# Gated mixing and dilated attention on one core: early constants, token-major values, ScalarE scales and one Newton chain per pair

## The chip, the cores and the metric

The kernel runs on one core of one Trainium2 chip. The metric is the device time of one launch in microseconds (us). A core has five instruction streams that run side by side and wait for each other by semaphores: PE (matmul, with its weight loads PEld), DVE (VectorE), ACT (ScalarE), POOL (GpSimd) and SP (SyncE, which issues the weight DMAs). Within a stream the instructions start in their written order, and that order is fixed when the program is built.

## The reference, cut to what matters

The program is two blocks of two layers each, on one sequence of 512 tokens and 1024 features in float32: a state-space mixer, a stick-breaking attention, a gated mixer with dilated attention ("even"), a gated linear attention, and a feed-forward part behind each. The change lies in the "even" mixer:

```python
u, v, q, k, vb = split(h @ w_in)                  # five parts of 512 columns each
vn = layer_norm_2(gelu(v))                        # gated mixing, chunks of 128 tokens
mixed = einsum('gts,bnsgc->bntgc', tril(w_s), vn) + b_s
a_out = gelu(u) * mixed
qh, kh, vh = rms_norm(heads(q), q_g), rms_norm(heads(k), k_g), heads(vb)   # 8 heads of 64
for window, dilation in ((128, 1), (512, 4), (2048, 16)):
    o_r, l_r = dilated_branch(qh, kh, vh, window, dilation)   # softmax attention on a strided band
o = sum(softmax over the three l_r) * o_r
return concatenate([a_out, o]) @ w_out
```

The three branches together are one softmax attention in which the weight of a key is multiplied by the number of branches that reach it (0 to 3).

## The kernel before, in words

The stages follow each other: ssm, ffn0, stick, ffn1, even, conv0, gla, conv1. In "even" everything is feature-major: `xh` and `xl` are the high and low parts of the activations, eight tiles of 128 features by 512 tokens, and a projection of 128 output features is 24 matmuls of 128x512 (`mm3`, L239 to L241: high by high, low by high, high by low for eight feature tiles). A projection of all 512 columns in token-major form is `token_proj` (L1190 to L1192): 96 matmuls of the same size, one PSUM bank for each of four blocks of 128 tokens. A weight block arrives by a DMA on SP's queue into `wr`, and is split into `wh` (ACT, L213) and `wl` (DVE, L214).

PSUM has eight banks: two for projections ("mm"), two for accumulations ("acc") and four for the rest ("aux"). Whoever writes into a bank waits until its last reader is done.

`gmlp` computes the gated mixing: `ev_v` by `token_proj`, four blocks of `ev_u`, gelu and layer norm of v (DVE L1234 normalises), the mixing matmuls (L1256 to L1258), ACT L1259, transposes L1263 and DVE L1264. It runs while the tail of ffn1 still finishes its layer norm (L382 to L464).

`dilated` first makes its constants: `dilated_masks` (the count `cnt` and the additive mask `dmask`, L1282 to L1295), the product `gqk` of the two norm gains from a small DMA (`gq`, L1302, L1304), `hsel` and `hrow`, and the zero columns of two value tiles. Then four pairs of heads follow. For each pair:

- `project(n=0)`, k: 24 matmuls; ACT L1322 squares; PE L1325 sums the squares per head (the moments); ACT L1338 copies k times `gqk`; DVE L1344 to L1347 is a chain of 13 small operations with `rstd` in it (three Newton steps), each on the result of the one before; PE L1354 transposes it; ACT L1356 copies (`rt`); PE L1358 broadcasts it; DVE L1359 multiplies; ACT L224 and DVE L225 split into `kh`, `kl`.
- `project(n=1)`, q: 24 matmuls, L1322, L1325, a split into `qh`, `ql` (L1017, L1018) and a Newton chain of its own, which ends in `rq` (L1350).
- `project(n=2)`, v: 24 matmuls and `values` (L1028, four transposes L1031, L1033, L1034).
- `scores` (S0, S1, S2; L1093, L1095): the 10 causal blocks of both heads of the pair, S0 being the largest query block; `weigh` (W, eight pieces of 512, 512, 128, 384, 128, 384, 256, 256 keys): DVE max (L1369), DVE `nb` (L1371), ACT exp (L1372), DVE times `cnt` with a row sum (L1373, called STT below), DVE reciprocal (L1374), DVE division (L1375); `transposed` (T: PE L1054, ACT L1059, DVE L1060); `av` (V: PE L1070 to L1075, ACT L1077, DVE L1078).

The order in which these steps are written is a table, `EVEN_STEPS`, which holds one round of the loop over the pairs; the number after the colon is the distance to the pair of the round. Under it a scheduler puts the instructions of each engine into the final order. "Linear matmuls" below are those of `mm3` and `token_proj`.

Of the kernel before, what the change touches and what calls it, by code (L numbers as in the profile page):

```python
# [8 lines left out]
F32 = mybir.dt.float32  # L9
F32R = mybir.dt.float32r  # L10
# [3 lines left out]
ALU = mybir.AluOpType  # L14
# [17 lines left out]
          + [("ba", 4), ("hg", 2)])  # L32
# [25 lines left out]
    "W01:0 S1:0 W00:0 W10:0 T01:-1 T00:0 T21:-1 V0:-2 P0:1 W11:0 S2:0 P2:0 V1:-1 W20:0 T11:0 T20:0 "  # L58
# [47 lines left out]
class Kern:  # L106
# [279 lines left out]
    def small(self, n=4, dt=F32):  # L386
        return self.nt("small", [P, n], dt, bufs=24)
# [633 lines left out]
    def values(self, ps, vz, scale=None):  # L1021
# [3 lines left out]
        if scale is None:  # L1025
            nc.scalar.activation(vt, ps, AF.Copy)
        else:
            nc.vector.tensor_mul(vt, ps, scale)  # L1028
# [7 lines left out]
    def value_tiles(self, n=2):
        res = []
        for k in range(n):
            t = self.pt(f"vz{k}", [P, 8, 192], F32R)
            self.nc.gpsimd.memset(t.bitcast(F32)[:, :, 0:64], 0.0)  # L1040
            res.append(t)
        return res
# [19 lines left out]
    def av(self, s, vz, wts, e):  # L1062
# [66 lines left out]
    def stick(self):  # L1129
        nc = self.nc  # L1130
        with self.phase("stick") as self.ph:
# [8 lines left out]
            vzs = self.value_tiles()  # L1140
# [54 lines left out]
    def gmlp(self, oh, ol):  # L1195
# [51 lines left out]
        self.linear(bu[len(pu):], self.xh, self.xl, lambda a, pss: evict(a + len(pu), pss))  # L1247

# [24 lines left out]
    def dilated_masks(self):  # L1273

        nc = self.nc
        ps = self.aux()
        for k, n in enumerate((4, 16)):
            a = self.scr()[0:n, :P]
            nc.gpsimd.memset(a, 0.0)
            nc.gpsimd.affine_select(a, a, pattern=[[0, P // n], [-1, n]], compare_op=ALU.not_equal, fill=1.0,  # L1280
                                    base=0, channel_multiplier=1)
            nc.tensor.matmul(ps[:, :P], a, a, start=k == 0, stop=k == 1)  # L1282
        cnt = self.pt("cnt")
        for j in range(4):
# [527 lines left out]
```

## Time and profile before

| | us |
|---|---|
| median of 3 runs (lowest, highest) | 2473.65 (2472.65, 2474.53) |
| the profiled execution | 2473.41 |
| its span in the trace | 2471.7 |
| PE busy over the span | 2405.6 (97%) |
| DVE busy over the span | 1415.8 (57%) |
| ACT busy over the span | 1005.5 (41%) |
| first scores of the four pairs (start of S0) | 1356.81, 1383.87, 1414.43, 1445.32 |
| first matmul of the stage behind "even" (L252) | 1509.18 |

The profiled execution is 1.7 us longer than its span, and 0.24 us under the median. A view by windows gives the busy time of each engine in a stretch; a view of waits gives what the idle time of an engine ended with; a timeline gives single instructions with start, duration, and in brackets the idle time ahead of them with its releaser.

### The profile page before, as it was taken

How to read it: one execution, taken by the hardware profiler on the slowest of the kernel's cores; microseconds unless marked ns; L12 is line 12 of the kernel's file. 1: busy time of each engine (PE TensorE's matmuls, PEld its weight loads, DVE VectorE, ACT ScalarE, POOL GpSimd, SP SyncE). 2: the span in 40 equal slices, each digit the busy share in tenths (PEclk: the TensorE clock that was granted, in tenths of full speed). 3: DMA queues.
4: the chain of work that ended last, by engine and by line, in shares of the span. 5: the costliest groups of instructions: out<-in, count | busy, mean ns of one | idle time of the engine just before them, and what ended most of it. 6: DMA issues, size and time to landing. Idle time of an engine off the chain costs nothing. (4 is left out here: it accounts for less than half of the span.)

```text
span 2471.7 us, 30857 instructions
## 1 busy us (share of the span) xinstructions
PE 2405.6 (97%) x12200; PEld 1993.5 (81%) x12204; DVE 1415.8 (57%) x2544; ACT 1005.5 (41%) x1542; POOL 14.0 (1%) x61
## 2 busy tenths in 40 slices
PE   5999999999999999999999999999999999999999
PEld 4888888888877798888877678888888787888888
DVE  9945633343777874333367886666435677656621
ACT  5843522222655643222244454333325454333321
POOL 0000000000000000000000000000000000000000
PEclk9999999999999999999999999999999999999999
DMA  3522222233211113223322112322332122222332
GB/s 90 110 95 93 79 101 100 95 94 96 77 60 60 43 61 119 97 99 88 102 92 72 48 43 86 111 99 97 94 93 86 55 86 77 94 94 99 93 111 64
DMA packets 99377, 213.50 MB, mean 86 GB/s; under 512 B 44528, under 2 KB 45168, under 8 KB 99232
## 3 DMA queue, kind: packets, MB, share of 16 engines
q1 hardware_dynamic: 99232, 211.53, 27.2%
q8 instruction: 96, 1.57, 0.3%
q14 instruction: 49, 0.40, 0.1%
HBM read 207.04 MB, written 2.10 MB: 85 GB/s over the span
## 5 line engine op out<-in xcount | busy, mean ns | idle before, releaser
L213 ACT ACTIVATE wh<-wr 128x1024 fp32r<-128x1024 f32 (+1 forms) x385 | 400.5, 1041 | 1014.4 <-PE mm L240 405.9
L214 DVE TENSOR_TENSOR wl<-wr,wh 128x1024 fp32r<-128x1024 f32 (+1 forms) x385 | 461.7, 1199 | 448.4 <-ACT wh L213 443.9
L239 PE MATMUL mm<-xh,wh 128*128 128x512 f32 x1016 | 398.9, 393 | 3.5 <-ACT scr L1338 3.1
L241 PE MATMUL mm<-xh,wl 128*128 128x512 f32 x1016 | 398.5, 392 | 0.0
L240 PE MATMUL mm<-xl,wh 128*128 128x512 f32 x1016 | 398.3, 392 | 0.0
L239 PE MATMUL acc<-xh,wh 128*128 128x512 f32 x760 | 296.7, 390 | 0.0
L240 PE MATMUL acc<-xl,wh 128*128 128x512 f32 x760 | 296.3, 390 | 0.0
L241 PE MATMUL acc<-xh,wl 128*128 128x512 f32 x760 | 296.0, 389 | 0.0
L239 PEld LDWEIGHTS mm<-xh,wh 128*128 128x128 f32 x1016 | 191.4, 188 | 44.9 <-ACT scr L1338 3.5
L240 PEld LDWEIGHTS mm<-xl,wh 128*128 128x128 f32 x1016 | 191.3, 188 | 39.5 <-issue 0.2
L241 PEld LDWEIGHTS mm<-xh,wl 128*128 128x128 f32 x1016 | 191.4, 188 | 39.0 <-issue 0.6
L240 PEld LDWEIGHTS acc<-xl,wh 128*128 128x128 f32 x760 | 143.0, 188 | 29.7 <-issue 0.2
L241 PEld LDWEIGHTS acc<-xh,wl 128*128 128x128 f32 x760 | 143.0, 188 | 29.5
L239 PEld LDWEIGHTS acc<-xh,wh 128*128 128x128 f32 x760 | 143.0, 188 | 29.4
L239 PE MATMUL mm<-hh,wh 128*128 128x512 f32 (+1 forms) x396 | 145.0, 366 | 1.0 <-DVE v L353 1.0
L239 PE MATMUL acc<-hh,wh 128*128 128x512 f32 (+1 forms) x396 | 145.1, 366 | 0.5 <-DVE v L353 0.5
L240 PE MATMUL acc<-hl,wh 128*128 128x512 f32 (+1 forms) x396 | 145.0, 366 | 0.0
L240 PE MATMUL mm<-hl,wh 128*128 128x512 f32 (+1 forms) x396 | 145.0, 366 | 0.0
L241 PE MATMUL acc<-hh,wl 128*128 128x512 f32 (+1 forms) x396 | 144.7, 365 | 0.0
L241 PE MATMUL mm<-hh,wl 128*128 128x512 f32 (+1 forms) x396 | 144.7, 365 | 0.0
L239 PEld LDWEIGHTS mm<-hh,wh 128*128 128x128 f32 x396 | 74.6, 189 | 13.6 <-DVE v L353 1.4
L239 PEld LDWEIGHTS acc<-hh,wh 128*128 128x128 f32 x396 | 74.6, 189 | 13.1 <-DVE v L353 0.9
(489 smaller groups left out, 3891.0 us busy)
## 6 DMA issues: line engine op xcount, KB each, us to landing
wr<-down_dram SPq DMA_DIRECT2D x64, 448.0 KB, 3.3
wr<-gu_g_dram SPq DMA_DIRECT2D x44, 512.0 KB, 3.2
wr<-gu_u_dram SPq DMA_DIRECT2D x44, 512.0 KB, 3.2
wr<-gate_dram SPq DMA_DIRECT2D x44, 512.0 KB, 3.2
wr<-up_dram SPq DMA_DIRECT2D x44, 512.0 KB, 3.2
wr<-down_dram SPq DMA_DIRECT2D x32, 512.0 KB, 3.6
wr<-sb_qkv_dram SPq DMA_DIRECT2D x24, 512.0 KB, 3.2
wr<-glu_dram SPq DMA_DIRECT2D x16, 512.0 KB, 3.3
```

The lines of the kernel that those rows point to most:

```text
L213: nc.scalar.activation(hi[:, :cols], raw[:, :cols], AF.Copy)
L214: nc.vector.tensor_sub(lo[:, :cols], raw[:, :cols], hi[:, :cols])
L239: nc.tensor.matmul(ps[:, c0:c1], wh[:, s], xh[k][:, c0:c1], start=st, stop=False)
L240: nc.tensor.matmul(ps[:, c0:c1], wh[:, s], xl[k][:, c0:c1], start=False, stop=False)
L241: nc.tensor.matmul(ps[:, c0:c1], wl[:, s], xh[k][:, c0:c1], start=False, stop=en)
```

## The change

- `even_consts` takes the place of `dilated_masks`: counts, mask, `hsel`, `hrow` and `gqk` are written ahead of `gmlp`, in tiles of their own; the gains come with the table of parameter columns that is loaded at the start of the program, so the DMA `gq` is gone.
- The values are projected token-major for all pairs at once, by `token_proj` of `ev_vb` in `gmlp` behind `ev_u` and ahead of the mixing (`even_values`), and are written straight into one tile `vz`. `project(n=2)`, its four transposes per pair and the step P2 are gone.
- In `gmlp` the normalisation of v goes from DVE to ACT (L1230), with one DVE operation more for its bias.
- In `weigh` the piece's `nb` and its final division go from DVE to ACT (L1374 and L1378 of the kernel after).
- The moments of k and q share a bank, and one Newton chain of 16 columns, behind q's moments, serves both; `rq` and `nrq` come by ACT (L1352, L1353).

```diff
 EVEN_STEPS = (
-    "W01:0 S1:0 W00:0 W10:0 T01:-1 T00:0 T21:-1 V0:-2 P0:1 W11:0 S2:0 P2:0 V1:-1 W20:0 T11:0 T20:0 "
+    "W01:0 S1:0 W00:0 W10:0 T01:-1 T00:0 T21:-1 V0:-2 P0:1 W11:0 S2:0 V1:-1 W20:0 T11:0 T20:0 "
     "W21:0 T10:0 P1:1 S0:1"
...
+        nb = self.small(4)
+        V.scalar_tensor_tensor(nb, ag[:, 0:8:2], -1.0, r, op0=ALU.mult, op1=ALU.mult)
         for n, v in enumerate(vg):
-            V.tensor_scalar(v, v, ag[:, 2 * n:2 * n + 1], r[:, n:n + 1], op0=ALU.subtract, op1=ALU.mult)
+            nc.scalar.activation(v, v, AF.Identity, scale=r[:, n:n + 1], bias=nb[:, n:n + 1])
...
         self.linear(bu[len(pu):], self.xh, self.xl, lambda a, pss: evict(a + len(pu), pss))
+        self.even_values()
...
+    def even_values(self):
+
+        nc = self.nc
+        pss = self.token_proj([("ev_vb", u) for u in range(4)], self.xh, self.xl)
+        for tb, ps in enumerate(pss):
+            r = self.rcol[:, tb:tb + 1]
+            src = ps.rearrange("p (n d) -> p n d", d=64)
+            h, l = (self.vz[:, tb, :, k:k + 64] for k in (64, 128))
+            nc.scalar.activation(h, src, AF.Copy, scale=r)
+            nc.vector.scalar_tensor_tensor(l, src, r, h, op0=ALU.mult, op1=ALU.subtract)
...
-            st = self.aux()
-            moments(ps, st, 0)
-            if n == 0:
-                kr = self.scr()
-                nc.scalar.activation(kr, ps, AF.Copy, scale=gqk)
-            else:
-                s["q"] = self.split_psum(ps, "q", 2)
-            var = self.small(8)
...
+            if n == 0:
+                s["st"] = self.aux()
+            moments(ps, s["st"], 8 * n)
+            if n == 0:
+                s["kr"] = self.scr()
+                nc.scalar.activation(s["kr"], ps, AF.Copy, scale=gqk)
                 return
+            s["q"] = self.split_psum(ps, "q", 2)
+            s["v"] = self.vz[:, :, 2 * hp:2 * hp + 2]
+            var = self.small(16)
...
-                V.scalar_tensor_tensor(nb, mx, -1.0, sc, op0=ALU.mult, op1=ALU.mult)
+                nc.scalar.activation(nb, mx, AF.Copy, scale=st["nrq"][:, 2 * qb + e:2 * qb + e + 1])
                 nc.scalar.activation(pq, zq, AF.Exp, scale=sc, bias=nb)
                 V.scalar_tensor_tensor(pq, pq, 1.0, cnt[:, T - kv:], op0=ALU.mult, op1=ALU.mult, accum_out=den)
                 V.reciprocal(den, den)
-                V.tensor_scalar(pq, pq, den, None, op0=ALU.mult)
+                nc.scalar.activation(pq, pq, AF.Copy, scale=den)
...
     def even(self):
-        with self.phase("evout") as self.op:
+        with self.phase("evout") as self.op, self.phase("evc") as self.ph2:
+            self.ph = self.ph2
             oh, ol = [None] * NM, [None] * NM
+            self.even_consts()
+            self.vz = self.pt("vz", [P, 4, 8, 192], F32R)
+            self.nc.gpsimd.memset(self.vz.bitcast(F32)[:, :, :, 0:64], 0.0)
```

The final order of the engines moves in three places that matter here. First ACT in the middle of the first pair, where the pieces of `weigh` follow each other; `aux` are score banks, `scr` the weights, L213 is a weight split and L1059 (L1051 after) a transposed copy. Before:

```order
L1372 ACTIVATE scr_11344<-aux_11214,small_11346,small_11151 128x128
L224 ACTIVATE kh_11340<-scr_11307 128x512
L1372 ACTIVATE scr_11344<-aux_11214,small_11355,small_11151 128x384
L1372 ACTIVATE scr_11373<-aux_11363,small_11375,small_11151 128x256
L1059 ACTIVATE wth_11383<-aux_11385 128x128
```

After, the same pieces:

```order
L1375 ACTIVATE scr_11386<-aux_11291,small_11388,small_11252 128x128
L1374 ACTIVATE small_11397<-small_11396,small_11253 128x1
L1378 ACTIVATE scr_11386<-scr_11386,small_11389 128x128
L1375 ACTIVATE scr_11386<-aux_11291,small_11397,small_11252 128x384
L1374 ACTIVATE small_11417<-small_11416,small_11253 128x1
L1378 ACTIVATE scr_11386<-scr_11386,small_11398 128x384
L1375 ACTIVATE scr_11415<-aux_11405,small_11417,small_11252 128x256
```

Between two exps (L1372 before, L1375 after) now stand the next piece's `nb` (L1374) and the division of the piece before (L1378), and the split of the next pair's k (L224) is no longer among them.

Second, DVE behind the last piece of the first pair: its STT (L1373 before, L1376 after), then the work for the next pair up to the first max (L1369, L1372). `ql` is the low part of q, `wtl` a transposed copy. Before:

```order
L1373 SCALAR_TENSOR_TENSOR scr_11399,small_11402<-scr_11399,cnt_10982 128x256
...
L1018 TENSOR_TENSOR ql_11457<-mm_11424,qh_11456 128x512
L1060 TENSOR_TENSOR wtl_11261<-aux_11409,wth_11260 128x3x128
L1344 TENSOR_TENSOR small_11460<-aux_11449,rsq_11003 128x8
...
L1347 TENSOR_TENSOR small_11478<-small_11478,cst_63 128x8
L1350 TENSOR_SCALAR small_11481<-small_11478 128x8
L1369 TENSOR_REDUCE small_11494<-aux_11484 128x1
```

After:

```order
L1376 SCALAR_TENSOR_TENSOR scr_11441,small_11444<-scr_11441,cnt_10484 128x256
L1347 TENSOR_TENSOR wide_11501<-aux_11377,small_11148 128x16
L1377 RECIPROCAL small_11444<-small_11444 128x1
L1348 TENSOR_SCALAR wide_11501<-wide_11501 128x16
L1020 TENSOR_TENSOR ql_11498<-mm_11466,qh_11497 128x512
...
L1350 TENSOR_TENSOR wide_11519<-wide_11519,cst_63 128x16
L1362 TENSOR_TENSOR scr_11384<-scr_11384,aux_11533 128x512
L225 TENSOR_TENSOR kl_11537<-scr_11384,kh_11536 128x512
L1372 TENSOR_REDUCE small_11551<-aux_11541 128x1
```

Before, only q's chain stood there, and k's chain, the product L1359 and the split L225 stood in the middle of the pieces; now the common chain, the product (L1362) and the split (L225) all stand between the last STT of one pair and the first max of the next.

Third, PE at the same place: transposes of the weights (L1054 before, L1046 after), the moments of the next q (L1325, L1330), and S0 of the next pair (L1095, L1087). Before:

```order
L1054 MATMUL aux_11394<-ident_58,scr_11373 128x128 x2
L1054 MATMUL aux_11409<-ident_58,scr_11241 128x128 x4
L241 MATMUL mm_11577<-xh_10215,wl_11574 128x512
L1325 MATMUL aux_11449<-hsel_10998,scr_11450 128x2 x4
L1095 MATMUL aux_11483<-kh_11340,qh_11456 128x512
```

After, with 12, 4 and 7 linear matmuls in the places left out:

```order
L1046 MATMUL aux_11436<-ident_58,scr_11415 128x128 x2
L1046 MATMUL aux_11451<-ident_58,scr_11318 128x128 x4
L1330 MATMUL aux_11377<-hsel_10513,scr_11491 128x2 x4
...
L1356 MATMUL aux_11526<-ident_58,wide_11519 2x128 x4
...
L1360 MATMUL aux_11533<-scr_11531,hrow_10514 128x512
...
L1087 MATMUL aux_11540<-kh_11536,qh_11497 128x512
```

The transposes of the chain (L1356) and the broadcast (L1360) of the next pair's k have moved from the middle of the pieces to the stretch between the last q moments and S0.

## Rows read from the trace of the kernel before

**Rows 1.** The page, busy time of the engines and share of the span.

```profile
PE 2405.6 (97%) x12200; PEld 1993.5 (81%) x12204; DVE 1415.8 (57%) x2544; ACT 1005.5 (41%) x1542; POOL 14.0 (1%) x61
```

**Rows 2.** Windows: length, busy PE, PEld, DVE, ACT, POOL, granted PE clock, DMA.

```profile
1285.00:1300.00 15.00, 12.94 (x55) 9.81 (x56) 14.46 (x35) 14.90 (x35) 0.00 (x0) 1.00 0.22 71
...
1339.00:1346.00 7.00, 3.57 (x20) 2.73 (x19) 5.03 (x17) 4.49 (x11) 2.62 (x8) 0.74 0.23 74
```

**Rows 3.** Windows cut at the four S0 and at the next stage's first matmul.

```profile
1356.81:1383.87 27.06, 25.61 (x136) 18.61 (x136) 20.85 (x79) 13.76 (x25) 0.00 (x0) 1.00 0.19 59
1383.87:1414.43 30.56, 29.43 (x162) 21.36 (x162) 25.77 (x94) 15.08 (x28) 0.00 (x0) 1.00 0.16 52
1414.43:1445.32 30.89, 29.95 (x164) 21.99 (x165) 26.66 (x95) 16.43 (x29) 0.00 (x0) 1.00 0.16 51
1445.32:1509.18 63.86, 61.39 (x295) 47.78 (x296) 46.96 (x111) 30.41 (x49) 0.00 (x0) 1.00 0.19 67
```

**Rows 4.** Waits of PE from 1290 to 1720: total, times, longest.

```profile
PE mm L239 <- ACT scr L1338: 3.1, 1, 3.1
PE aux L1054 <- DVE scr L1375: 2.3, 2, 1.3
...
PE aux L411 <- DVE acc L464: 1.1, 1, 1.1
```

**Rows 5.** Timeline of PE behind the longest wait: start, duration, instruction.

```profile
1345.64 0.63 PE L240 MATMUL mm<-xl,wh 128*128 128x512 f32 x1
...
1349.06 0.43 PE L239 MATMUL mm<-xh,wh 128*128 128x512 f32 x1
```

**Rows 6.** Timeline of PE in a run of linear matmuls, 21 starts apart.

```profile
1312.09 0.39 PE L241 MATMUL acc<-xh,wl 128*128 128x512 f32 x1
...
1316.86 0.39 PE L241 MATMUL acc<-xh,wl 128*128 128x512 f32 x1
```

**Rows 7.** Timeline of DVE, first pair: STT of pieces 1, 4, 5, 8.

```profile
1361.97 0.69 DVE L1373 SCALAR_TENSOR_TENSOR scr<-scr,cnt 128x512 f32<-128x512 f32 x1 [2.19 <-ACT scr L1372]
...
1368.29 0.55 DVE L1373 SCALAR_TENSOR_TENSOR scr<-scr,cnt 128x384 f32<-128x384 f32 x1
...
1375.24 0.28 DVE L1373 SCALAR_TENSOR_TENSOR scr<-scr,cnt 128x128 f32<-128x128 f32 x1
...
1381.98 0.41 DVE L1373 SCALAR_TENSOR_TENSOR scr<-scr,cnt 128x256 f32<-128x256 f32 x1
```

**Rows 8.** Timeline of DVE, Newton chain of the second pair's q, 12 starts apart.

```profile
1385.99 0.16 DVE L1345 TENSOR_SCALAR small<-small 128x8 f32<-128x8 f32 x1
...
1388.39 0.17 DVE L1350 TENSOR_SCALAR small<-small 128x8 f32<-128x8 f32 x1
```

**Rows 9.** Groups of DVE by line and shape, 1340 to 1460: busy, mean ns.

```profile
L1369 DVE TENSOR_REDUCE small<-aux 128x1 f32<-128x512 f32 x8 | 5.5, 684 | 0.0
L1371 DVE SCALAR_TENSOR_TENSOR small<-small,small 128x1 f32<-128x1 f32 x29 | 4.5, 155 | 0.1
```

**Rows 10.** Groups of ACT by line and shape, 1340 to 1460.

```profile
L1372 ACT ACTIVATE scr<-aux,small,small 128x512 f32<-128x512 f32 x8 | 6.2, 777 | 16.5 <-DVE small L1371 16.5
...
L1372 ACT ACTIVATE scr<-aux,small,small 128x128 f32<-128x128 f32 x8 | 3.6, 455 | 13.6 <-DVE small L1371 13.6
...
L1338 ACT ACTIVATE scr<-mm,gqk 128x512 f32<-128x512 f32 x4 | 2.8, 692 | 2.1 <-DVE small L1345 2.1
L224 ACT ACTIVATE kh<-scr 128x512 fp32r<-128x512 f32 x4 | 2.5, 632 | 4.8 <-DVE scr L1359 4.8
...
L1356 ACT ACTIVATE rt<-aux 2x512 f32<-2x512 f32 x4 | 2.3, 584 | 4.0 <-PE aux L1354 4.0
...
L1372 ACT ACT_TABLE_LOAD x1 | 1.3, 1283 | 2.3 <-DVE small L1371 2.3
L1285 ACT ACTIVATE cnt<-aux 128x128 f32<-128x128 f32 x4 | 0.9, 278 | 0.4 <-PE aux L1282 0.4
```

**Rows 11.** Timeline of DVE in ffn1's tail: the low split of the mixing weights.

```profile
1279.12 1.23 DVE L225 TENSOR_TENSOR wsl<-wsr,wsh 128x1024 fp32r<-128x1024 f32 x1
```

More of the change, by code (lines that the diff above doesn't have):

```diff
@@ L1019, in split_psum, with values @@
         return hi, lo
-    def values(self, ps, vz, scale=None):
+    def values(self, ps, vz):
         nc = self.nc
         vt = self.scr()
-        if scale is None:
-            nc.scalar.activation(vt, ps, AF.Copy)
-        else:
-            nc.vector.tensor_mul(vt, ps, scale)
+        nc.scalar.activation(vt, ps, AF.Copy)
         tr = self.aux()
@@ L1032, in values @@
         src = tr.rearrange("p (b d) -> p b d", d=64)
+        vz = vz.rearrange("p t e d -> p (t e) d")
         nc.scalar.activation(vz[:, :, 64:128], src, AF.Copy)
         nc.vector.tensor_sub(vz[:, :, 128:192], src, vz[:, :, 64:128])
[L1036 to L1042, printed above, removed]
     def new_wt(self):
@@ L1271, in out_pair, with even_consts @@
         return h, l
-    def dilated_masks(self):
+    def even_consts(self):
         nc = self.nc
[L1276 to L1284, printed above, removed]
-            nc.scalar.activation(cnt[:, j * P:(j + 1) * P], ps[:, :P], AF.Copy, bias=1.0 if j == 3 else 0.0)
-        own = cnt[:, 3 * P:]
-        nc.gpsimd.affine_select(own, own, pattern=[[-1, P]], compare_op=ALU.is_ge, fill=0.0, base=0,
-                                channel_multiplier=1)
-        near = self.scr()[:, :P]
-        nc.gpsimd.memset(near, 1.0)
-        nc.gpsimd.affine_select(near, near, pattern=[[1, P]], compare_op=ALU.is_ge, fill=0.0, base=0,
-                                channel_multiplier=-1)
-        nc.vector.tensor_add(cnt[:, 2 * P:3 * P], cnt[:, 2 * P:3 * P], near)
-        mask = self.pt("dmask", [P, T], BF16)
-        nc.vector.tensor_scalar(mask, cnt, 0.5, -1e30, op0=ALU.is_lt, op1=ALU.mult)
-        return cnt, mask
@@ new lines, in even_consts @@
+        cnt, mask = self.pt("cnt"), self.pt("dmask", [P, T], BF16)
+        with self.phase("evt") as ph:
+            ps = self.aux()
+            near = ph.tile([P, P], F32, name=self.nm("near"), tag="near", bufs=1)
+            nc.gpsimd.memset(near, 1.0)
+            nc.gpsimd.affine_select(near, near, pattern=[[1, P]], compare_op=ALU.is_ge, fill=0.0, base=0,
+                                    channel_multiplier=-1)
+            for k, n in enumerate((4, 16)):
+                a = ph.tile([P, P], F32, name=self.nm("sel"), tag="sel", bufs=2)[0:n]
+                nc.gpsimd.memset(a, 0.0)
+                nc.gpsimd.affine_select(a, a, pattern=[[0, P // n], [-1, n]], compare_op=ALU.not_equal, fill=1.0,
+                                        base=0, channel_multiplier=1)
+                nc.tensor.matmul(ps[:, :P], a, a, start=k == 0, stop=k == 1)
+            for j in range(4):
+                nc.scalar.activation(cnt[:, j * P:(j + 1) * P], ps[:, :P], AF.Copy, bias=1.0 if j == 3 else 0.0)
+            own = cnt[:, 3 * P:]
+            nc.gpsimd.affine_select(own, own, pattern=[[-1, P]], compare_op=ALU.is_ge, fill=0.0, base=0,
+                                    channel_multiplier=1)
+            nc.vector.tensor_add(cnt[:, 2 * P:3 * P], cnt[:, 2 * P:3 * P], near)
@@ new lines, in even_consts @@
+        nc.vector.tensor_scalar(mask, cnt, 0.5, -1e30, op0=ALU.is_lt, op1=ALU.mult)
+        hsel, hrow, gqk = self.pt("hsel", [P, 2]), self.pt("hrow", [2, P]), self.pt("gqk", [P, 1])
+        nc.gpsimd.memset(hsel, 0.0)
+        for e in (0, 1):
+            nc.gpsimd.memset(hsel[64 * e:64 * e + 64, e:e + 1], 1.0 / 64)
+        nc.gpsimd.memset(hrow, 0.0)
+        nc.gpsimd.affine_select(hrow, hrow, pattern=[[-1, 2], [0, 64]], compare_op=ALU.not_equal, fill=1.0,
+                                base=0, channel_multiplier=1)
```

64 lines of the change are left out of this document (27 added, 37 removed).

## The prediction

> **What bounds the kernel now.** The page first: PE is busy 97% of the span, DVE 57%, ACT 41% [rows 1]. So a change can gain at most what PE still waits, and it can lose wherever it makes PE wait. Next the windows of the stage: in the four attention pairs PE is busy 25.6 of 27.1, 29.4 of 30.6 and 29.9 of 30.9 us, and 61.4 of 63.9 in the last stretch [rows 3]. Then the list of waits: the one long wait is 3.1 us for the copy of k (ACT L1338), which needs `gqk` and so the DMA of the gains [rows 4]. Behind it the granted clock is low: 0.74 over 1339 to 1346 [rows 2], and eight matmul starts take 3.42 us, 0.43 each [rows 5], the lower of the two levels (1.2 GHz), against (1316.86 - 1312.09)/21 = 0.227 in a run at the upper one, 2.4 GHz [rows 6]. Some nine matmuls at 0.2 too much are 1.8 us.
>
> The point that decides comes last: PE is nearly full in the pairs because the projections of the coming pair, 72 matmuls of 0.227 = 16.3 us, fill it while DVE and ACT work off the softmax. That softmax is a chain of its own. In the first pair it runs from S0 at 1356.81 to the STT of piece 1 at 1361.97 (5.2 us), to that of piece 8 at 1381.98 (20.0 us) and to the next S0 at 1383.87 (1.9 us) [rows 3, 7]. PE and this chain take about the same time; whoever shortens one alone gains nothing, and whoever lengthens one pays.
>
> **Early constants and gains.** The wait of 3.1 us and the 1.8 us of low clock behind it have no cause any more: `gqk` is there long before. Gain 4.9. The mixing no longer waits for v's normalisation, since 96 matmuls lie ahead of it: 0.3 at most, taken.
>
> The same edits put work into ffn1's tail. By the order, the splits of the mixing weights (1.23 us on DVE [rows 11], about as much on ACT) move from ahead of the layer norm's last chain to 1285 to 1300, where DVE is busy 14.46 and ACT 14.90 of 15 us [rows 2]; L411, which there ends a 1.1 us wait for DVE L464 [rows 4], comes that much later. `cnt` and `dmask` stand inside the chain ahead of it, each at most a 512-wide operation (0.69). The chain itself starts earlier by the split that left. Together I take 1.6, between -0.5 (all of it hidden, the chain early) and +2.5 (all of it on the path). The memset of `vz` and the selects on POOL wait for nobody that PE needs before the first S0; if that cover were gone they would cost a few us once.
>
> **Values in one go.** `token_proj` puts 96 matmuls, 21.8 us, ahead of the first S0. By the order the first S0 moreover has 31 more matmuls of k1 and q1 ahead of it and 24 (v of pair 0) fewer: 103 in all, 103 x 0.227 = 23.4 us. Four transposes fewer are 0.4. The chain from q's moments to S0 of the first pair is covered by only about 20 matmuls now: 0.8. So the first S0 moves by 23.4 - 4.9 - 0.3 - 0.4 + 1.6 + 0.8 = **+20.2 us**. This is no loss as long as the pairs get shorter by the same amount: 3 x 24 value matmuls leave them (16.3 us), and 31 of the next pair's go ahead (7.0). DVE L1028 and L1034 go too.
>
> **The pieces of `weigh`.** From one STT to the next the order now demands STT, max of the next piece, its `nb` on ACT, the division of this piece on ACT, the next exp. For two 512-wide pieces: STT 0.69 [rows 7], max 0.68 [rows 9], `nb`, division 0.69 (as L1338, which also reads a column as scale), exp 0.78 [rows 10]: 2.84 without `nb`. `nb` on ACT is not in the trace; it lies between DVE's 0.16 [rows 9] and ACT's 128 x 128 copy with a further 0.1 for the column operand, 0.38 (L1338 against 0.59 to 0.6 for plain 512-wide copies such as L1356 [rows 10]); one column being far from 128, I take 0.22. So 3.06. For the other widths I take the lines between the 512 and the 128 rows (STT and max 0.55, 0.41, 0.28; exp 0.67, 0.56, 0.46; division 0.59, 0.48, 0.38): 2.33, 2.10, 2.10, 2.10, 2.33, 2.08. Seven steps: **16.1 us**. With `nb` and division left on DVE, the latter off the chain, the same sum is 12.9. In the trace the seven took 20.0, of which 6.95 went between pieces 4 and 5 [rows 7], where the order had k's Newton chain on DVE and its copy `rt` on ACT ahead of the exp. That work leaves the pieces. The other six took 1.8 more than their sum (a weight split in between); I take 0.7 of it again, from 0 to 1.8: 16.8.
>
> A rule of the Trainium skill bears on `nb`. The page "ScalarE: Activation LUTs" ("What ACT_TABLE_LOAD costs") gives an activation 186 ns, plus 93 ns for a column operand; that estimate is 0.28, and by it 28 pieces would be 1.7 us longer than by mine.
>
> **One Newton chain per pair.** In the order it stands behind the last STT, since q's moments (PE) do, and everything up to S0 hangs on it: q's moments behind the last transposes 1.0; 13 operations of 0.20 [rows 8] with `ql` and two `wtl` pieces among them, 4.0; four small transposes 0.7; `rt` 0.58 [rows 10]; the broadcast, one fp32 matmul of 512, as four passes of 0.227: 1.0 (this and the transposes are estimates from rows 6); the product 0.68; `kh` 0.63 [rows 10]; five hand-overs of 0.1. Sum **9.1 us** where the trace has 1.9. From 7 (nothing else between) to 11 (a weight split of 1.2 and a wait for it). What saved 13 operations on DVE saves none on this path: k's chain lay inside the pieces, beside their waits.
>
> **The pairs.** S0 to the first STT stays 5.2 in the first pair and is 3.9 in the others, which have no table load (1.28 [rows 10]). Pair 1: 5.2 + 16.8 + 9.1 = 31.1. Pair 2: 3.9 + 16.8 + 9.1, and 1.8 for a weight split and the copies of the pair before on the path: 31.6. Pair 3, with 1.0 of these: 30.8. Together 93.5 against 88.5 [rows 3]: **+5.0**, although PE has 23 us less to do there. PE waits some 10 us per pair.
>
> **The last stretch.** 3.9 + 16.8 to the last STT, 5.7 for its division, transposes, copies, values and output split, then by the order about 154 linear matmuls (35.0): 61.4 against 63.9, **-2.4**.
>
> **Sum.** 20.2 + 5.0 - 2.4 = 22.8; on the profiled execution's 2473.4 (0.24 under the median, which changes nothing) this is **2496 us**, slower by 0.9%. The bounds, `nb` on both ends included, give 2486 to 2506.
>
> **Rivals.** *PE keeps the bound* (faster). If the chain fits beside PE's work, the pairs cost what PE does in them: 85.0 busy [rows 3] - 16.3 - 7.0 = 61.6 instead of 88.5, and the time is 2473.4 + 20.2 + 61.6 - 88.5 = 2467. It decides from 22.8 us per pair downward ((88.5 - 20.2)/3). For it: DVE is busy only 20.9 to 26.7 us per pair [rows 3] and loses about 7 of that. Against it: 16.1 for the pieces and 7 for the k chain are already more, and they stand in a row. This is also what a rule of the skill would make of it: "Perfetto Trace Analysis" ("Optimizing Scalar/DVE Operations") recommends handing work to Scalar if DVE is saturated. Here DVE has idle time, and the pieces wait on single results. The same section speaks for breaking instructions up where engines that are not saturated make bubbles elsewhere, which is the reverse of one 16-wide chain; by that rule the forecast stands. Chance 0.10.
>
> *The k chain hides* (no change). If moments and chain slip between the pieces, 3 us remain of the 9.1, the pairs take about 75, and 20.2 + 75 - 88.5 - 2.4 = +4.3 with the bounds of the pieces gives 2470 to 2478. For it: q's matmuls are done early. Against it: the order on DVE. Chance 0.09.
>
> *The clock falls in every pair* (slower still). PE's waits are then longer than the 3.1 us that went with a low clock here; at 1.8 each for three pairs 2501, with more falls up to 2508. For it: rows 5. Against it: matmuls stand between the waits. Chance 0.20.
>
> *The change is not what it says*: the order shows each part at its place. Chance 0.01.
>
> **How the numbers follow.** Forecast 0.60, the rivals 0.10, 0.09, 0.20, 0.01. Predicted is the forecast's 2496. The range leaves out the PE bound and the lower half of the hidden chain below and little above: 2477 to 2508. A measurement can tell about 0.2% from no change, 2469 to 2478. Faster: 0.10; same: 0.08, nearly all of the hidden chain; slower: 0.82.
>
> **What would show it.** Right: the wait for the k copy and the low clock at 1342 gone; first S0 near 1377; S0 to S0 near 31 us with PE busy about 21 of it; DVE idle between the STTs ending on ACT; DVE's 16-wide chain behind the last STT and PE idle there for several us. Wrong: S0 to S0 under 25 us, or the STTs of a pair under 14 us from first to last, or the common chain finished before the last STT. A first S0 after 1380 would blame the constants in ffn1's tail; a granted clock under 0.9 in the pairs speaks for the third rival.

## The result and the profile after

The changed kernel takes 2515.3 us (median of 4 runs, 2510.8 to 2525.5) against 2473.8: 1.0176 times the time of before, 95% interval 1.0152 to 1.0200. I had forecast slower, 2496 in a range of 2477 to 2508. The direction held; the loss is 41 us where I had 22, and lies outside the range. Executions of one kernel lie up to 15 us apart and a trace shows only one of them: for after, e7, e13 and e15 one that is 4 to 5 us under the kernel's median, for e1, e2, e3, e5 and e10 one that is 3 to 7 us over it.

The profiled execution took 2510.82 us, 37.4 more than that of before. Its windows, cut as [rows 3] are, show where (columns as there: length, busy PE, PEld, DVE, ACT, POOL, granted PE clock, DMA):

```profile
1375.99:1413.26 37.27, 30.34 (x128) 21.42 (x129) 16.71 (x57) 19.13 (x41) 0.00 (x0) 0.82 0.10 32
1413.26:1447.90 34.64, 27.67 (x139) 19.84 (x139) 18.53 (x60) 20.09 (x44) 0.00 (x0) 0.95 0.09 31
1447.90:1483.56 35.66, 27.20 (x120) 18.77 (x122) 17.95 (x61) 18.51 (x43) 0.00 (x0) 0.81 0.04 16
1483.56:1549.36 65.80, 56.63 (x252) 44.33 (x254) 39.80 (x78) 33.92 (x63) 0.00 (x0) 0.87 0.17 56
```

The first S0 starts 19.2 us later than before (1375.99 against 1356.81). The three pairs take 107.6 us instead of 88.5, the last stretch 65.8 instead of 63.9. That is 40.2 at the first matmul of the next stage; 2.8 come back behind it. DVE's busy time per pair fell from between 21 and 27 us to between 17 and 19, as intended, and the granted clock fell from 1.00 to 0.82, 0.95, 0.81 and 0.87. PE is busy 85.2 us in the three pairs, as before (85.0), though the records show 387 matmuls there instead of 462: a part of them ran at the lower clock.

The list of PE's waits follows, in the same stretch as [rows 4] (total, times, longest). The copy of k is gone from it, and in its place stands the division of the weights on ACT (L1378), for which the transposes (L1046) wait:

```profile
PE aux L1046 <- ACT scr L1378: 21.1, 8, 4.4
PE aux L1087 <- ACT kh L224: 2.9, 2, 1.4
PE mm L239 <- DVE ql L1020: 2.8, 3, 1.1
...
PE aux L413 <- DVE acc L466: 2.2, 1, 2.2
```

The next lines are from the timeline of DVE in the first pair: the STT (L1376) of pieces 1, 2, 7 and 8, the first operation of the common Newton chain, and the product for the next k (they answer to [rows 7]):

```profile
1380.93 0.69 DVE L1376 SCALAR_TENSOR_TENSOR scr<-scr,cnt 128x512 f32<-128x512 f32 x1 [2.51 <-ACT scr L1375]
...
1383.87 0.69 DVE L1376 SCALAR_TENSOR_TENSOR scr<-scr,cnt 128x512 f32<-128x512 f32 x1 [1.57 <-ACT scr L1375]
...
1394.32 0.43 DVE L1376 SCALAR_TENSOR_TENSOR scr<-scr,cnt 128x256 f32<-128x256 f32 x1 [1.25 <-ACT scr L1375]
...
1401.09 0.41 DVE L1376 SCALAR_TENSOR_TENSOR scr<-scr,cnt 128x256 f32<-128x256 f32 x1
...
1403.59 0.17 DVE L1347 TENSOR_TENSOR wide<-aux,small 128x16 f32<-128x16 f32 x1 [2.08 <-PE aux L1330]
...
1411.53 0.69 DVE L1362 TENSOR_TENSOR scr<-scr,aux 128x512 f32<-128x512 f32 x1 [4.25 <-PE aux L1360]
```

Six of the seven steps of this pair take 13.4 us together; I had 14.0. The seventh takes 6.8, where I had 2.1. (In the second pair the fourth step takes 4.8, in the third the fifth 5.7 and the seventh 4.0.) ACT's timeline shows what it waits for: the division of piece 7 (L1378) stands behind a copy of transposed weights (L1051) and a weight split (L213), and the copy waits 3.5 us for PE:

```profile
1397.82 0.28 ACT L1051 ACTIVATE wth<-aux 128x128 fp32r<-128x128 f32 x1 [3.53 <-PE aux L1046]
1398.06 1.06 ACT L213 ACTIVATE wh<-wr 128x1024 fp32r<-128x1024 f32 x1
1399.02 0.49 ACT L1378 ACTIVATE scr<-scr,small 128x256 f32<-128x256 f32 x1
```

And PE's timeline shows why it is late there. It stood 3.3 us for the division of piece 2, then ran moments, scores and linear matmuls at the low clock (two starts 0.43 apart), and the transposes that ACT waits for stand behind those matmuls:

```profile
1385.78 0.66 PE L1046 MATMUL aux<-ident,scr 128*128 128x128 f32 x4 [3.29 <-ACT scr L1378]
...
1390.85 0.63 PE L240 MATMUL mm<-xl,wh 128*128 128x512 f32 x1
1391.28 0.63 PE L241 MATMUL mm<-xh,wl 128*128 128x512 f32 x1
...
1397.30 0.49 PE L1046 MATMUL aux<-ident,scr 128*128 128x128 f32 x3
```

Two windows give the clock: the place of [rows 2] is at the full clock now, and inside the first pair it is 1.2 GHz for most of 8 us.

```profile
1339.00:1346.00 7.00, 7.00 (x33) 5.79 (x32) 2.45 (x2) 2.92 (x3) 0.00 (x0) 1.00 0.30 85
1386.00:1394.00 8.00, 7.83 (x29) 5.68 (x28) 4.23 (x18) 5.93 (x16) 0.00 (x0) 0.58 0.20 66
```

So ACT waits for PE, which waited for ACT, and each round is made longer by the clock that the wait brings. The 2.8 us that come back later go with a low stretch that the trace of before has near 1935 (0.72 over 1930 to 1942) and this one has not.

### The profile page after: what moved, and what is told of

Its sections match the earlier page's. It is cut to its first block, busy times and chain, and to the rows that moved or that the text cites. A ratio compares the mean times of both kernels' runs of the same rounds, so it can differ in the third digit from the quotient of the medians.

```text
span 2509.1 us, 30756 instructions
## 1 busy us (share of the span) xinstructions
PE 2419.3 (96%) x12184; PEld 2004.0 (80%) x12188; DVE 1393.8 (56%) x2417; ACT 1030.6 (41%) x1618; POOL 14.6 (1%) x60
## 5 line engine op out<-in xcount | busy, mean ns | idle before, releaser
L213 ACT ACTIVATE wh<-wr 128x1024 fp32r<-128x1024 f32 (+1 forms) x385 | 400.4, 1041 | 1024.4 <-PE mm L240 413.4
L214 DVE TENSOR_TENSOR wl<-wr,wh 128x1024 fp32r<-128x1024 f32 (+1 forms) x385 | 461.7, 1200 | 460.2 <-ACT wh L213 456.1
L239 PE MATMUL mm<-xh,wh 128*128 128x512 f32 x984 | 387.5, 394 | 2.3 <-DVE ql L1020 1.9
L240 PE MATMUL mm<-xl,wh 128*128 128x512 f32 x984 | 386.1, 392 | 0.0
L241 PE MATMUL mm<-xh,wl 128*128 128x512 f32 x984 | 385.5, 392 | 0.0
L239 PEld LDWEIGHTS mm<-xh,wh 128*128 128x128 f32 x984 | 185.9, 189 | 43.0 <-DVE ql L1020 2.1
L241 PEld LDWEIGHTS mm<-xh,wl 128*128 128x128 f32 x984 | 185.6, 189 | 39.4 <-issue 1.9
L240 PEld LDWEIGHTS mm<-xl,wh 128*128 128x128 f32 x984 | 185.8, 189 | 39.0 <-issue 0.8
L239 PEld LDWEIGHTS mm<-hh,wh 128*128 128x128 f32 x396 | 74.7, 189 | 13.5 <-DVE v L353 1.4
L239 PEld LDWEIGHTS acc<-hh,wh 128*128 128x128 f32 x396 | 74.6, 188 | 13.1 <-DVE v L353 0.9
```

What stands on the lines that cost most here:

```text
L213: nc.scalar.activation(hi[:, :cols], raw[:, :cols], AF.Copy)
L214: nc.vector.tensor_sub(lo[:, :cols], raw[:, :cols], hi[:, :cols])
L239: nc.tensor.matmul(ps[:, c0:c1], wh[:, s], xh[k][:, c0:c1], start=st, stop=False)
L240: nc.tensor.matmul(ps[:, c0:c1], wh[:, s], xl[k][:, c0:c1], start=False, stop=False)
L241: nc.tensor.matmul(ps[:, c0:c1], wl[:, s], xh[k][:, c0:c1], start=False, stop=en)
```

## The experiments

Each kernel's ratio is to runs of the kernel before on the same chip (medians 2472.9 to 2474.0). "After" with a part undone, or "before" with one thing added.

### One part at a time

**e1**: the kernel before with the constants early.

```diff
+            self.even_consts()
...
-        cnt, mask = self.dilated_masks()
-        gq = self.load("gq", [P, 2], i["ev_qkg"], eng=nc.sync, pool=self.ph)
+        cnt, mask, hsel, hrow, gqk = self.evc
```

> The kernel before, with its constants and the product of the gains made early and nothing else changed (values, scales, Newton chains, normalisation as before). If the early constants do what the prediction says, the wait of 3.1 us for the k copy and the low clock behind it (1.8) go and ffn1's tail costs 1.6: 2473.8 - 3.3 = 2470.5, faster by 0.13%. Rival: the work in ffn1's tail eats the whole gain, 2473 to 2476, with the wait at L413 1.5 us longer or more.

2475.4 us, 1.0018 (1.0008 to 1.0028). The gain that I had booked isn't there. The wait for the k copy is gone. The trace has new low stretches in the first two pairs (0.87 and 0.85), and they take 32.0 and 33.9 us instead of 27.1 and 30.6; but the trace took 2481.8 us, 6.4 over the median, so what takes the gain at the median is not shown.

**e2**: after, with `nb` and division on DVE again.

```diff
-                nc.scalar.activation(nb, mx, AF.Copy, scale=st["nrq"][:, 2 * qb + e:2 * qb + e + 1])
+                V.scalar_tensor_tensor(nb, mx, -1.0, sc, op0=ALU.mult, op1=ALU.mult)
...
-                nc.scalar.activation(pq, pq, AF.Copy, scale=den)
+                V.tensor_scalar(pq, pq, den, None, op0=ALU.mult)
```

> The kernel after with nb and the division of weigh back on DVE; values early and the common Newton chain stay. If the two ACT operations per piece lengthen the chain of the pieces and block ACT's queue, the seven steps fall from 20.2 (1380.93 to 1401.09 in the first pair) to 14 to 15 us and the time to 2515 - 4 x 5 = 2495. Rival (the common chain and the lost value matmuls are what costs, and the pieces only move the idle time): 2508 to 2515.

2517.7 us, 1.0191 (1.0172 to 1.0209). My first reading of the trace after, that ACT's two operations per piece make the loss, falls: without them the seven steps take 20.1 to 25.0 us in the four pairs, and the time is the same.

**e3**: after, with a Newton chain each for k and q. **e4**: after, with the values per pair.

```diff
-            var = self.small(16)
+            var = self.small(8)
...
-            r = self.rstd(var, 16)
+            r = self.rstd(var, 8)
```

> The kernel after with a Newton chain each for k and q as before; scales on ACT and values early stay. If the common chain is what stands between the last piece and the next S0, that stretch falls from 12.2 us (1401.09 to 1413.26) to 3 or 4, and k's chain goes into the pieces: 3 x 8 saved, some 3 x 3 given back there, about 2500. Rival (PE at the low clock and ACT's queue set the stretch): within 4 us of 2515.

2498.2 us, 1.0109 (1.0094 to 1.0125): 17 us back, as expected. From the last STT to the next S0 it is 3.5, 3.4 and 3.5 us, and the seven steps take 22.1, 26.0 and 23.4, together 9.9 more than in after. The edit also gives k's and q's moments a bank each again, so it doesn't part the chain from the shared bank.

```diff
-        self.even_values()
...
+            if n == 2:
+                s["v"] = vzs[hp % 2]
+                self.values(ps, s["v"], self.rrow)
+                return
```

> The kernel after with the values projected per pair as before, inside the attention; scales on ACT and the common chain stay. If PE merely lacks work in the pairs, the 72 value matmuls fill its idle time again: first S0 near 1358, pairs still 31 to 36 us, clock near 1.0, time 2515 - 23 - 6 (clock) = 2486. Rival (the chain and its queues grow with the values' four transposes and copies on ACT and DVE): pairs of 38 us and more, 2495 to 2505.

2495.2 us, 1.0093 (1.0078 to 1.0108): 20 us back, but by the rival's way. The first S0 goes back to 1353.1, the clock doesn't recover (0.95, 0.72 and 0.92), and the pairs take 35.9, 41.7 and 40.5.

### Do the parts add up?

**e5** undoes e3's and e4's parts together, **e6** keeps only the values (and early constants), **e7** only the common chain. The edits are those above.

> Undoes two parts at once: values per pair and a Newton chain each for k and q, as before; scales on ACT, early constants and the normalisation on ACT stay. If the costs of the early values (2515 - 2495 = 20) and of the common chain (2515 - 2498 = 17) add up, 2515 - 37 = 2478. If they are one cost with two names (either alone makes the pairs a chain with PE idle), undoing both brings little more than undoing one: 2488 to 2494.

2473.6 us, 1.0009 (1.0000 to 1.0019).

> Early constants, early values and the normalisation on ACT alone: the scales of weigh are on DVE and k and q have a Newton chain each, as before. The price of the early values by themselves. If they only pay for PE work that the pairs can't get back (21.8 us into the front, chain of 30 us per pair unchanged): 2475 + 20 = 2495. Rival: without ACT's two operations per piece the pairs shorten to 25 us, since PE has 16 us less to do in them: 2480.

2496.8 us, 1.0102 (1.0087 to 1.0118).

> Early constants, the common Newton chain and the normalisation on ACT; values per pair and scales on DVE as before. The price of the common chain by itself. If it stands on the path behind the last piece: 2475 + 3 x 5 to 6 = 2492. Rival (it costs only where ACT's scales block the queue too): 2475 to 2480.

2492.7 us, 1.0088 (1.0071 to 1.0104).

With after and e1 to e4 that is every combination of three parts (all have the early constants, and all but e1 the normalisation on ACT):

| scales on ACT | values early | common chain | us |
|---|---|---|---|
| no | no | no | 2475.4 (e1) |
| yes | no | no | 2473.6 (e5) |
| no | yes | no | 2496.8 (e6) |
| no | no | yes | 2492.7 (e7) |
| yes | yes | no | 2498.2 (e3) |
| yes | no | yes | 2495.2 (e4) |
| no | yes | yes | 2517.7 (e2) |
| yes | yes | yes | 2515.3 (after) |

The values cost 20 to 25 us in every pair of rows that differ in them alone, the chain 17 to 22, the scales between -2.4 and +2.5, and the costs add up within 3 us. In e6 the pairs take 31.0, 34.5 and 33.6 us, in e1, with 72 more matmuls in them, 32.0, 33.9 and 31.8: PE's work leaves the pairs and the pairs don't notice. (The granted clock of these pairs is 0.88, 0.80 and 0.75 in e6, and 0.87, 0.85 and 1.00 in e1, so a lower clock may be a part of the reason; the table doesn't part the two.) In e7 the eight STTs take 17.9, 18.0 and 27.0 us from first to last (e1: 24.2, 26.1 and 24.7), but from the last STT to the next S0 it is 11.8, 13.5 and 9.5 (e1: 3.6, 2.2 and 2.2).

### More and less work for PE

**e8**: after, with a fourth product in the projections of k and q. **e9**: after, without their third product (the weights' low part doesn't enter k and q). **e13**: the fourth product twice. **e12**: the fourth product in the kernel before.

```diff
-            ps, = self.group([(bk, bq)[n][hp]], self.xh, self.xl)
+            w = (bk, bq)[n][hp]()
+            ps = self.mm()
+            (wh, wl), k0, nk = w[0]
+            self.mm3(ps, w, self.xh, self.xl, last=False)
+            for j in range(nk):
+                c = slice(j * P, (j + 1) * P)
+                nc.tensor.matmul(ps, wl[:, c], self.xl[k0 + j], start=False, stop=j == nk - 1)
```

> The kernel after with a fourth product in the projections of k and q (low weights by low activations, 8 more matmuls each): 64 more matmuls, 14.5 us of PE work, 28 of them (6.4 us) ahead of the first S0 and the rest in the pairs. If the pairs are a chain of ACT and DVE with idle PE, only the 6.4 us show, less whatever the fuller PE wins at the clock: 2515 to 2522. If PE or its place in the queues sets the pairs, all shows: 2530 or more.

2508.8 us, 1.0160 (1.0138 to 1.0183): with 14.5 us more work for PE no slower. The median is 6 us lower, but the intervals overlap. The first S0 starts where that of after does (1375.97), so nearly all of the 64 matmuls stand in the pairs (442 matmuls recorded there, 387 in after), and not 28 of them ahead as I had expected. Windows from S0 to S0:

```profile
1375.97:1410.09 34.12, 32.10 (x158) 22.48 (x159) 17.93 (x58) 18.87 (x41) 0.00 (x0) 1.00 0.14 47
1410.09:1443.53 33.44, 31.07 (x156) 22.95 (x156) 18.30 (x60) 19.61 (x44) 0.00 (x0) 0.95 0.09 32
1443.53:1481.63 38.10, 30.73 (x128) 21.60 (x128) 18.07 (x61) 19.11 (x44) 0.00 (x0) 0.78 0.04 15
```

> The kernel after with the third product (low weights by high activations) of the k and q projections left out, so 64 fewer matmuls, 14.5 us less PE work, 6.4 of it ahead of the first S0. Mirror of e8. If PE's work in the pairs is free either way: 2515 - 6 = 2509. If the granted clock is what e8 won back, the emptier PE falls more often: pairs of 36 us and more, 2512 to 2520 in spite of the shorter front. If PE's work were on the path: 2500.

2514.0 us, 1.0166 (1.0152 to 1.0180): with 14.5 us less work for PE no faster. Its first pairs, windows from S0 to S0:

```profile
1375.34:1414.43 39.09, 27.25 (x100) 17.79 (x100) 16.01 (x56) 18.89 (x41) 0.00 (x0) 0.66 0.07 26
1414.43:1452.18 37.75, 29.77 (x122) 20.56 (x122) 19.16 (x61) 18.98 (x43) 0.00 (x0) 0.73 0.10 34
1452.18:1488.02 35.84, 29.38 (x121) 19.94 (x121) 17.25 (x60) 18.29 (x43) 0.00 (x0) 0.71 0.03 10
```

> The kernel after with the low-by-low product of k and q taken twice, 128 more matmuls than after, 29 us of PE work, 13 of them ahead of the first S0. After plus 14.5 us (e8) was 6 us faster, after minus 14.5 us (e9) the same. If pairs with idle PE cost by the low clock, this again hides all but the part ahead of the first S0: 2508 to 2516. If e8 was luck of the order: 2523 and more.

2513.3 us, 1.0161 (1.0147 to 1.0176): 29 us more work for PE, and the time of after. The same windows:

```profile
1380.28:1412.94 32.66, 32.08 (x161) 22.91 (x160) 16.59 (x57) 19.06 (x41) 0.00 (x0) 1.00 0.10 33
1412.94:1446.01 33.07, 32.35 (x169) 23.61 (x169) 18.30 (x60) 19.34 (x43) 0.00 (x0) 1.00 0.10 32
1446.01:1479.44 33.43, 31.55 (x162) 22.28 (x161) 18.99 (x62) 19.41 (x44) 0.00 (x0) 1.00 0.10 33
```

The instructions of the chain on ACT and DVE are the same in these kernels. With PE kept busy they run at the full clock and a pair takes 33 us (34.1 and 33.4 in the first two of e8); with an emptier PE the clock is down for much of the time and a pair takes 35.8 to 39.1 (38.1 in the third of e8), though PE has less to do. In e13 PE is busy 94 to 98% of the pairs, so its own work may hold them at 33 us; then the chain alone would be shorter still. The Trainium skill's page "Perfetto Trace Analysis" ("Matmul Optimizations") says that the matmul engine scales its power with its use, so that matmuls should come back to back; these traces agree as far as the granted clock shows it, 0.66 to 0.73 with the least work and 1.00 with the most.

> Control for e8: the kernel before with the same fourth product in the projections of k and q, 64 more matmuls, 14.5 us of PE work. Before, PE is nearly full in the pairs, so most of it must show: 2473 + 11 to 15 = 2484 to 2488. If the pairs of the kernel before were set by the ACT and DVE chain as well, only the part ahead of the first S0 (some 4 to 6 us) shows: 2477 to 2480.

2479.4 us, 1.0028 (1.0018 to 1.0037): 5.4 us for 14.5 us of work, the rival's number, but not by the rival's way. Windows cut as [rows 3] are:

```profile
1353.22:1380.90 27.68, 26.53 (x141) 19.03 (x141) 21.35 (x81) 14.08 (x24) 0.00 (x0) 1.00 0.15 51
1380.90:1413.31 32.41, 32.07 (x172) 23.57 (x171) 25.10 (x91) 14.97 (x26) 0.00 (x0) 1.00 0.12 39
1413.31:1449.19 35.88, 35.64 (x182) 26.03 (x182) 28.44 (x97) 16.37 (x29) 0.00 (x0) 1.00 0.13 45
1449.19:1515.24 66.05, 65.98 (x312) 52.16 (x312) 47.55 (x111) 31.35 (x51) 0.00 (x0) 1.00 0.20 72
```

The three pairs take 7.5 us more than before and the last stretch 2.2, together 9.7; the 50 more matmuls recorded there are 11.3 us of work (50 x 0.227). So in the pairs of the kernel before PE's work does show, as its busy time says. What hides is the part ahead of the first S0, which comes 3.6 us earlier in spite of it: in this order PE no longer waits for the copy of k (its list of waits has none), and the trace shows no low clock in the stage at all. The added matmuls have covered the wait by themselves.

### Where the booked gain of the early gains goes

**e10**: the kernel before, the norm gains from the parameter columns.

```diff
...
-        gq = self.load("gq", [P, 2], i["ev_qkg"], eng=nc.sync, pool=self.ph)
         gqk = self.pt("gqk", [P, 1])
-        V.tensor_mul(gqk, gq[:, 0:1], gq[:, 1:2])
+        V.tensor_mul(gqk, self.qg, self.kg)
```

> The kernel before with one edit: the two gains come with the parameter columns, so the DMA that the k copy waits for is gone; constants stay where they were. If the prediction's reading holds, the wait of 3.1 us and the 1.8 us of low clock go and nothing lands in ffn1's tail: 2473 - 4.9 = 2468, down to 0.2% faster. Rival: as in e1 the freed time is given back at the low clock and in longer pairs: 2472 to 2476.

2474.4 us, 1.0012 (1.0002 to 1.0022). The wait is gone, and the order of the attention moves a little with it: a weight split (L213, L214) now stands ahead of the STT of piece 7, PE waits 3.0 us at the end of the first pair, and the low clock that was at 1342 is at 1384 to 1400. The trace took 2480.1 us, 5.7 over the median; but the lowest of the eleven times, 2472.5, shows no gain of 4.9 either. Windows of the first two pairs and the wait:

```profile
1357.96:1389.06 31.10, 26.34 (x132) 18.80 (x131) 21.69 (x84) 14.42 (x24) 0.00 (x0) 0.93 0.16 52
1389.06:1421.95 32.89, 32.71 (x159) 23.41 (x158) 25.07 (x93) 14.43 (x26) 0.00 (x0) 0.86 0.09 33
```

```profile
PE aux L1054 <- DVE scr L1374: 4.3, 2, 3.0
```

**e11**: e10 with the scales on ACT (edit as in e2, reversed).

> e10 with the scales of weigh (nb and the division) on ACT. In e5 against e1 these scales brought 2 us although they lengthen the sum of a pair's steps. Same here: 2 us under e10. If they cost as my sum of the steps says (16.1 against 12.9 us per pair), with PE nearly full behind it: 2 to 6 us over e10.

2476.8 us, 1.0010 (1.0001 to 1.0018): no difference from e10 that could be told.

**e14** to **e18** put work for PE where the clock of e5 and e10 falls. e14 is e10 with e8's product everywhere; in the others it is taken for the second pair alone, whose k and q are projected during the first pair's softmax (in e18 for q alone):

```diff
...
+            more = n < 2 and hp == 1
+            self.mm3(ps, w, self.xh, self.xl, last=not more)
+            for j in range(nk if more else 0):
```

> e10 (gains from the parameter columns) with the fourth product for k and q. e10 lost what it won to a new stretch at the low clock at the end of the first pair; e12 had none in the stage and cost 5 us. If the clock takes e10's gain, this one stays at the upper clock and is e12 minus the wait, 2479.4 - 4.9 = 2474.5; if the pairs give it back by the chain, 2479.

2480.1 us, 1.0032 (1.0021 to 1.0044): the time of e12. It says nothing on the clock, since e12 had no wait for the copy of k left that the early gains could take away.

> e10 with the fourth product for k and q of the second pair alone, which are projected while the first pair's softmax runs: 16 matmuls, 3.6 us of PE work where e10 has its low clock. If that work keeps the clock up, the 6.8 us at half clock (3.4 of work) are won for what it costs: 2470 to 2474. If it goes on top: 2478.

2472.6 us, 0.9995 (0.9986 to 1.0004). The pairs take 27.9, 30.7 and 31.8 us at clock 1.00, where e10 had 31.1, 32.9 and 31.3; but these two traces took 2468.6 and 2480.1 us, while the medians differ by 1.8. (The 6.8 us of the expectation are what the two windows of e10 lack to the full clock, 0.07 of 31.1 and 0.14 of 32.9, and not the length of the low stretch.)

> e5 (early constants, normalisation and scales on ACT, values per pair, two Newton chains) with the same 16 matmuls for the second pair. e5 too has its one low stretch of the attention at the end of the first pair. Same two cases: 2469 to 2473, or 2477.

2468.5 us, 0.9986 (0.9976 to 0.9995).

> e16 without the early constants and with the normalisation on DVE: the kernel before with the gains from the parameter columns, scales on ACT and the 16 filling matmuls for the second pair. If e16's gain is the removed wait at the upper clock plus the scales, and the early constants only cost in ffn1's tail (L413 waits 1.1 us either way in e16), this one is as fast or 1 us faster: 2467 to 2469. If the early constants carry a part, 2471 to 2473.

2472.1 us, 0.9997 (0.9988 to 1.0006).

> e16 with half the filling, only in the second pair's q (8 matmuls, 1.8 us). If 8 are enough to keep the clock up at the end of the first pair: 2466 to 2468. If not, the low stretch of e5 is back: 2473 to 2475.

2465.7 us, 0.9972 (0.9959 to 0.9985), the fastest of all and 50 us under the kernel after. Windows from S0 to S0:

```profile
1351.07:1378.93 27.86, 27.15 (x141) 19.89 (x142) 18.31 (x66) 18.72 (x41) 0.00 (x0) 0.96 0.17 57
1378.93:1409.81 30.88, 28.95 (x160) 21.11 (x160) 22.64 (x77) 20.55 (x46) 0.00 (x0) 1.00 0.16 51
1409.81:1441.29 31.48, 30.49 (x166) 22.19 (x167) 23.84 (x79) 22.06 (x47) 0.00 (x0) 1.00 0.15 51
```

e5 with 8 redundant matmuls is 8 us faster than e5, in whose first two pairs the clock was 0.92 and 0.87 (in a trace 3.5 us over its median). This fits the reading that the clock takes the gain of the removed wait and 1.8 us of work keep it; it isn't shown, since the same 8 matmuls were not tried at a place without a low clock, where they would move the order alone. Not all of e18's 8 us can be the clock: its last stretch is 62.4 us long, e16's 65.3, and the orders of the two differ there too. Without the early constants (and with the normalisation on DVE) e17 is 3.6 us behind e16, with overlapping intervals, and has low stretches between 1342 and 1356, up to the first S0; that the early constants are worth something beside the fill is not shown by this.

## Why the prediction was wrong

**Direction and place: right.** The loss comes about as worked out: the value matmuls go ahead of the first S0, the pairs don't get shorter, and the common chain stands between the last piece and the next S0. e6 shows the first two (pairs as long with 72 matmuls fewer), e7 and the table the third. On the profiled execution the loss is 37.4 against my 22.8: -1.0 at the first S0, +14.1 in the pairs, +4.3 in the last stretch and -2.8 behind it. In the pairs the seven steps are 11.0 over the forecast, the way from the last STT to the next S0 6.2 over, and that from S0 to the first STT 3.2 under.

**The first S0: right.** Forecast +20.2, measured +19.2. This is the sum; its terms were not measured one by one.

**The price of a step on ACT: right.** `nb` on ACT is 0.29 us long, and the next instruction of ACT starts 0.2 us behind it (1390.92 and 1391.12 in the first pair). Its line, over 1375 to 1500:

```profile
L1374 ACT ACTIVATE small<-small,small 128x1 f32<-128x1 f32 x29 | 8.5, 292 | 21.2 <-DVE small L1372 21.2
```

I had 0.22 in the sum; the estimate of 0.28 that the Trainium skill's page "ScalarE: Activation LUTs" ("What ACT_TABLE_LOAD costs") leads to is close to the instruction's length in this trace. In the first pair six of the seven steps came out 0.07 to 0.12 under the forecast each.

**The pieces: the step that failed.** "I take 0.7 of it again, from 0 to 1.8: 16.8." Measured 20.2, 19.1 and 22.2 in the three pairs. I had summed instructions that wait on each other's results and taken a small allowance for the other work in the queues. What stands in ACT's queue ahead of a division or an exp is not only work of a known length: a transposed copy and a weight split wait for PE, and PE for ACT. That closed circle could be seen in the order. It is not the two ACT operations of each piece that make it: in e2, without them, the seven steps take 22.8, 25.0 and 23.3 us. The allowance was also read from the first pair alone. The same trace of before has, in the second and third pair, these STTs of pieces 1, 4, 5 and 8:

```profile
1390.25 0.69 DVE L1373 SCALAR_TENSOR_TENSOR scr<-scr,cnt 128x512 f32<-128x512 f32 x1 [0.91 <-ACT scr L1372]
...
1396.19 0.56 DVE L1373 SCALAR_TENSOR_TENSOR scr<-scr,cnt 128x384 f32<-128x384 f32 x1
...
1402.43 0.29 DVE L1373 SCALAR_TENSOR_TENSOR scr<-scr,cnt 128x128 f32<-128x128 f32 x1
...
1412.19 0.42 DVE L1373 SCALAR_TENSOR_TENSOR scr<-scr,cnt 128x256 f32<-128x256 f32 x1
...
1419.37 0.69 DVE L1373 SCALAR_TENSOR_TENSOR scr<-scr,cnt 128x512 f32<-128x512 f32 x1 [0.91 <-ACT scr L1372]
...
1427.85 0.55 DVE L1373 SCALAR_TENSOR_TENSOR scr<-scr,cnt 128x384 f32<-128x384 f32 x1
...
1433.46 0.29 DVE L1373 SCALAR_TENSOR_TENSOR scr<-scr,cnt 128x128 f32<-128x128 f32 x1
...
1443.09 0.42 DVE L1373 SCALAR_TENSOR_TENSOR scr<-scr,cnt 128x256 f32<-128x256 f32 x1
```

Without the step from piece 4 to 5 the other six take 15.7 and 18.1 us there, against 13.1 in the first pair: by my own sum an excess of about 4.4 and 6.8, where I had bounded it by 1.8.

**The clock: the second step.** I gave the clock's fall in the pairs a chance of 0.20 as a case of its own, at 1.8 us for each of three pairs. It belonged in the forecast: I had forecast 10 us of waits per pair, against one wait of 3.1 us ahead of the low clock in the kernel before. e13 gives its size: same chain, full clock, 99.2 us for the three pairs, against 107.6. So of the 14.1 us by which the pairs exceed my 93.5, some 8.4 go with the clock, and 5.7 remain at the full one, which I put down to the queues without having measured them by themselves (and PE's own work in e13 may be a part of them). The three windows lack 15.2 us to the full clock (0.18 of 37.3, 0.05 of 34.6, 0.19 of 35.7), so about half of what the clock withheld shows in the time.

**From the last STT to the next S0:** forecast 9.1, measured 12.2, 11.9 and 9.4, and 9.7 to 10.2 at the full clock of e13. A fair sum: of the 6.2 us that it is short of in three pairs, 3.6 are gone in e13. A low clock isn't needed for a longer way, though: in the first pair of e7, at a clock of 1.00, it is 11.8 us.

**The last stretch: wrong sign**, -2.4 forecast, +1.9 measured. Here too the clock is down (0.87), and no coming pair is left to project that could fill PE; what each of the two costs was not measured.

**The gain of the early constants: wrong.** "The wait of 3.1 us and the 1.8 us of low clock behind it have no cause any more ... Gain 4.9." In the sum of after it was hidden by the loss, but e1 and e10 show that alone it isn't had: +0.18% and +0.12%. In the traces of e1 and e10 (2481.8 and 2480.1 us) what is late next is the end of the first pair, with a low clock of its own; e18 fits that, and the cause at the median stays open.

**The rivals.** That PE keeps the bound, and that the chain hides, are both excluded (e6, e7). The third, the falling clock, came true in its condition (0.82 and 0.81 in two pairs) and at a higher price than its 1.8 us per pair. Two of my ranges were added up too narrowly: the bounds of the terms reach from 2483 to 2512 and not from 2486 to 2506, and for the hidden chain +4.3 with the bounds of the pieces doesn't lead down to 2470. The rule for breaking up instructions in the Trainium skill's page "Perfetto Trace Analysis" ("Optimizing Scalar/DVE Operations"), which I had beside the first rival, fits: one 16-wide chain in place of two costs 17 to 22 us. The same section's advice to hand work to Scalar is for a saturated DVE, while here DVE is busy 77 to 86% of the pairs before, and the scales are worth -2.4 to +2.5 us in four comparisons.

**What stays open.** Every edit moves the scheduler's order a little everywhere in the attention (e10 against before is one example), so comparisons of two kernels within some 3 us don't tell the edit from the order. How the 5.7 us divide among single queue entries wasn't tried, and the gain of e18 has no control for the order.

## What to carry to other kernels

Work that fills PE beside a chain of ACT and DVE is worth its place there: moved ahead of the chain it cost its whole length here, because the chain stayed as long. Before you merge two small chains into a wide one, look where each stood: one that ran beside other work for nothing and now waits for the later of its inputs has moved onto the path. And if a forecast has PE wait in a loop as long as it did ahead of a low clock elsewhere in the trace, put the low clock into the sum; a few redundant matmuls in the wait may be cheaper than the wait. Take an allowance for waits from all rounds of the loop, not from the first, and check a number that fits a rival against the stretches of the trace: in e12 it fitted for another reason.

## What the runs showed of the hardware

Added PE work made the kernel after no slower: +14.5 us of matmuls gave 2508.8, +29 us 2513.3, -14.5 us 2514.0, against 2515.3. The granted clock of its three pairs went with it: 0.66 to 0.73 with the least work, 0.81 to 0.95 as changed, 1.00, 0.95 and 0.78 with 14.5 us more, 1.00 with the most. In the kernel before, whose PE is nearly full in the pairs, 14.5 us of added work cost 5.4, since a part of it filled a wait of 3.1 us and the low clock behind that was gone; and e18, with 8 added matmuls, takes 0.28% less than that kernel.
